# Latent attention heads in an order written by hand, modulation weights loaded a step ahead, zeros written by GpSimd

## The chip, the cores and the metric

The kernel runs on one core of a Trainium2 chip. The metric is the device time of that core in microseconds (us), from one launch to its end. The kernel before took 2492.16 us as the median of three runs (2489.03 to 2494.43).

Four engines share the work and run their own instruction streams side by side: TensorE (PE in the profile; its weight loads are listed as PEld), VectorE (DVE), ScalarE (ACT) and GpSimd (POOL). SyncE (SP) issues nearly all DMAs of this kernel, one after the other, in one queue. An engine works through its own stream in order and waits on semaphores for results of the others.

## The reference, cut to what matters

The program is a backbone of two layers over 256 latent tokens (x) and 256 context tokens (ctx) of width 2048, all in float32. Layer 0 has eight neighbourhood attention heads and eight latent attention heads side by side; layer 1 is a gated DeltaNet. The change lies in layer 0, in the last neighbourhood head, the latent heads, and the part of layer 1's modulation that is computed among them.

```python
def na_mla_layer(x, ctx, c, c_ctx, w_mod, b_mod, norm, w_in, rpb, q_norm, w_qb, kv_norm, w_kvb, w_out, update_ctx):
    ...
    hx = modulate(x, norm, sh[:, None], sc[:, None]) @ w_in
    hc = modulate(ctx, norm, sh_c, sc_c) @ w_in
    ...
    def mla_q(cq_t):                       # rank 512 -> 8 heads of 128 + 64 (rotary part)
        q = to_heads(rmsnorm(cq_t, q_norm) @ w_qb, MLA_HEADS)
        return q[..., :MLA_NOPE_DIM], q[..., MLA_NOPE_DIM:]
    def mla_kv(ckv_t):                     # rank 512 -> 8 heads of 128 (keys) + 128 (values)
        kv = to_heads(rmsnorm(ckv_t, kv_norm) @ w_kvb, MLA_HEADS)
        return kv[..., :MLA_NOPE_DIM], kv[..., MLA_NOPE_DIM:]
    ...
    o_mla = mla_latent_attention(qn, rope_2d(qr), kn, v=v, kr=rope_2d(kr), kn_c=kn_c, kr_c=kr_c, v_c=v_c)
    y = (jnp.concatenate([merge_heads(o_na), merge_heads(o_mla)], axis=-1) * jax.nn.silu(z)) @ w_out
def adaln_params(cond, w_mod, b_mod):      # shift, scale, gate of a layer
    return jnp.split(jax.nn.silu(cond) @ w_mod + b_mod, 3, axis=-1)
```

A latent head's score is the product of its 128 own channels plus the product of 64 rotary channels, whose keys all heads share. The latent queries attend to all 512 keys, the context queries to the 256 context keys alone.

## The kernel before

**Tiling.** T = 512 tokens (256 latent, 256 context) stand on the free axis, channels on the 128 partitions. A float32 product is made of three fp32r matmuls: high by high, high by low, low by high. `dense` issues them (L90, L91, L92), `split` makes the two parts of a weight tile (ScalarE's cast L77, VectorE's subtraction L78), and `product` (L365) is the same for scores and values. Weight tiles of 128x1024 (512 KB) are loaded by `load_raw` into a ring of four, and split into rings of three.

**A head** (`attend`): four transposes of v (pv, L371), then for the latent and the context queries, two blocks of 128 each: scores sp (L365), for a neighbourhood head a bias (L387), their maximum (L389), the exponential (L392) that also leaves the sum, its reciprocal and the scaling (L394, L395), transposes of the probabilities (pt, L398), the split of these into PT (high part on ScalarE, L357, low part on VectorE, L358), and the values po (L365), which are multiplied into the gate `go` (L405). PSUM holds two tiles "mm" for dense products, two "sp", a ring of two called "tr" that pv, pt and pp (the rotary permutation) share, one "st" (po) and one "pm" (pmod, pmt).

**The stage of the change.** After seven neighbourhood heads the kernel makes `craw` (the latent queries' and keys' inputs of rank 512 each) and the rotary keys, and the queries, keys and values of neighbourhood head 7 (`na7`). From `craw` it makes `cx`: high parts by ScalarE (L468) and low parts by VectorE (L469), eight of 128x512 each; `ch` is its first half. `cx` takes the memory of `hx`, the input of the dense products until then. Its second half, `qr`, holds the rotary queries of all latent heads, 64 partitions a head; the other 64 partitions are set to zero by ScalarE, as a copy of ones times 0 (L481, eight of 64x1024). Then come head 7's attention, four rotary blocks (`dense` of the weights `ab_wqr`, two tiles; then `roped`, L444 to L457: copy, permutation pp, three VectorE steps, two splits) and the eight latent heads 8 to 15, each with three dense products of 12 matmuls from 1536 columns of `ab_wb`, two tiles a head (queries and keys, 1024; values, 512). The tiles are called W0 and W1 (`ab_wqr`), W2 and W3 (head 8), W4 and W5 (head 9) and so on.

**The modulation.** Layer 1's modulation weights come as `mraw` tiles of 512 KB. Chunks 2, 3 and 8 have four groups each; a group is four matmuls (L141) of 32 rows of cond each, which write the four quarters of pmod and read two `mraw` tiles. The 12 groups are steps of a generator (`ahead`); the pool of its tiles is opened when `craw` has been freed. Chunk 9 follows behind the last dense product, and then comes the output projection.

**What sets the order.** The stage is written as straight code, and the framework's scheduler puts each engine's instructions into an order by its own estimate of times. Only the later DeltaNet stage has an order by hand (`manual_schedule`).

Of the kernel before, what the change touches and what calls it, by code (L numbers as in the profile page):

```python
# [8 lines left out]
F32 = mybir.dt.float32  # L9
F32R = mybir.dt.float32r  # L10
AF = mybir.ActivationFunctionType
# [6 lines left out]
S = 256  # L18
# [8 lines left out]
def trunk_kernel(ctx: ExitStack, tc: tile.TileContext, g):  # L27
# [10 lines left out]
    def mm_tile():  # L38
        return mmp.tile([128, T], F32, name="mm", tag="mm")
# [41 lines left out]
    def load_split(src, n=2048):  # L81
        return [split(load_raw(src[:, c:min(n, c + 1024)], min(1024, n - c)), min(1024, n - c))
                for c in range(0, n, 1024)]

    def dense(ps, w, off, kt, xh, xl, k0=0, sl=slice(0, T), first=True, last=True):
        for k in range(kt):
            c = off + k * 128
            wh, wl = w[c // 1024]
            c = slice(c % 1024, c % 1024 + 128)
            PE.matmul(ps, wh[:, c], xh[:, k0 + k, sl], start=first and k == 0, stop=False)  # L90
            PE.matmul(ps, wh[:, c], xl[:, k0 + k, sl], start=False, stop=False)  # L91
            end = PE.matmul(ps, wl[:, c], xh[:, k0 + k, sl], start=False, stop=last and k == kt - 1)  # L92
        return end.ins
# [225 lines left out]
    with tc.tile_pool(name="ab", bufs=2, reuse_waits="tile") as tp, \  # L319
# [87 lines left out]
        def keep(p, name):  # L407
            t = tp.tile([128, T], F32, name=name, tag=name, bufs=1)
            A.copy(t, p)
            return t  # L410
# [58 lines left out]
                V.tensor_tensor(ch[:, 8 + j], craw[:, j], ch[:, j].bitcast(F32), op=ALU.subtract)  # L469
        cr.release()  # L470
        mr = tc.alloc_tile_pool(name="mr2", bufs=2, reuse_waits="tile")
        ahead = later(mr, ((1, (2, 3, 8), 0),))

        rows = slice(0, 64), slice(64, 128)
        attend(*na7)
        w = load_split(g["ab_wqr"])
        for j in range(4):
            p = mm_tile()
            dense(p, w, j * 512, 4, ch, ch[:, 8:])
            for e in range(2):  # L480
                A.activation(qr[rows[1 - e], 4 * j + 2 * e:4 * j + 2 * e + 2],  # L481
                             ones[rows[1 - e], 0:1].unsqueeze(2).broadcast_to([64, 2, T]), AF.Copy, scale=0.0)
            roped(p, MLA_SCALE, [(rows[e], *[qr[rows[e], 4 * j + 2 * e + i] for i in range(2)]) for e in range(2)])
        for h in range(8):
            w = load_split(g["ab_wb"][h], 1536)
            o = []
            for j, (k0, name, sc) in enumerate(((0, "qT", MLA_SCALE), (4, "kT", 1.0), (4, "vT", 1.0))):
                p = mm_tile()
                last_mm = dense(p, w, j * 512, 4, ch, ch[:, 8:], k0)
                o.append(keep(p, name) if name == "vT" else parts(p, name, scale=sc))  # L490
            steps(ahead, 1)
# [948 lines left out]
```

## Time and profile before

| | busy us | share of the span | instructions |
|---|---|---|---|
| TensorE matmuls (PE) | 2428.2 | 97% | 16110 |
| TensorE weight loads (PEld) | 1963.1 | 79% | 16110 |
| VectorE (DVE) | 1762.8 | 71% | 3538 |
| ScalarE (ACT) | 1105.6 | 44% | 2446 |
| GpSimd (POOL) | 161.1 | 6% | 165 |

| | |
|---|---|
| median of 3 runs | 2492.16 us |
| profiled execution, its own time | 2493.04 us |
| its span, first to last instruction | 2491.2 us |
| HBM read, written | 356.94 MB, 35.39 MB |

A row of a group of instructions reads: line, engine, operation, result<-operands, the tile's partitions by elements, and the count; then busy us, mean ns of one, and the idle time of the engine ahead of them with what ended most of it. A row of the timeline begins with the start and the length in us; in brackets stands the wait ahead of it and what ended it. The whole span has one core, and its latent stage is the stretch from some 687 to 901 us.

### The profile page before, as it was taken

What the parts mean: (1) busy time and instruction counts of PE and PEld (TensorE: products, weight loads), DVE (VectorE), ACT (ScalarE), POOL (GpSimd) and SP (SyncE); (2) the same over time, 40 slices, a digit from 0 to 9 for tenths busy, and PEclk for the clock granted to TensorE, in tenths of its full rate; (3) what the DMA queues carried; (4) which work ended last, traced back from release to release, by engine and by line L of the source; (5) the groups of instructions that cost most, each with busy time, mean ns of one, the idle gap of its engine ahead of it and who ended that gap; (6) DMA issues with size and microseconds to landing.
All of it is one profiled execution on the core that took longest, in us unless ns stands there. A gap on an engine that the chain in (4) does not pass through costs nothing.

```text
span 2491.2 us, 42483 instructions
## 1 busy us (share of the span) xinstructions
PE 2428.2 (97%) x16110; PEld 1963.1 (79%) x16110; DVE 1762.8 (71%) x3538; ACT 1105.6 (44%) x2446; POOL 161.1 (6%) x165
## 2 busy tenths in 40 slices
PE   6999999999989999999999999999999999999998
PEld 4557888888858878858998989987777777777787
DVE  4654678883356687856998988885777777777765
ACT  4223332333254432257565655634444544445453
POOL 0000000000000000020011101000000000012000
PEclk9999999999999999999999999999999999999999
DMA  8872645542253366664665666774343333336454
GB/s 252 282 277 87 200 154 172 169 157 84 88 187 110 102 198 204 226 210 136 195 173 158 179 178 180 204 201 108 87 116 103 115 112 98 106 100 184 148 193 141
DMA packets 254940, 397.24 MB, mean 159 GB/s; under 512 B 122257, under 2 KB 163857, under 8 KB 254609
## 3 DMA queue, kind: packets, MB, share of 16 engines
q1 hardware_dynamic: 253584, 393.00, 52.0%
q8 instruction: 127, 2.08, 0.3%
q10 hardware_dynamic: 1152, 1.54, 0.2%
q14 instruction: 77, 0.62, 0.1%
HBM read 356.94 MB, written 35.39 MB: 157 GB/s over the span
## 4 chain that ended last, share of the span: by engine, by line
PE 88%; issue 5%; DMA 3%; DVE 2%; ACT 1%; SPq 0%; POOL 0%; DVEq 0%; POOLq 0%; ACTq 0%
PE mm L90 21%; PE mm L91 20%; PE mm L92 20%; PE pks L1033 3%; PE pmod L141 3%; PE ptr L1045 2%; PE sp L365 2%; PE mm L105 2%; PE po L365 1%; DMA mraw<-dn_wm 1%; PE ptr L1078 1%; PE psu L1064 1%; PE pks L1064 1%; PE pt L398 1%; PE mm L107 1%
## 5 line engine op out<-in xcount | busy, mean ns | idle before, releaser
L90 PE MATMUL mm<-hx,whi 128*128 128x512 f32 (+1 forms) x2304 | 843.7, 366 | 2.3 <-ACT t L664 2.2
L91 PE MATMUL mm<-hx,whi 128*128 128x512 f32 (+1 forms) x2304 | 820.6, 356 | 2.5 <-issue 2.5
L92 PE MATMUL mm<-hx,wlo 128*128 128x512 f32 (+1 forms) x2304 | 819.4, 356 | 0.6 <-DVE wlo L78 0.6
L77 ACT CAST whi<-raw 128x1024 fp32r<-128x1024 f32 (+2 forms) x346 | 338.6, 980 | 701.4 <-PE mm L91 502.3
L78 DVE TENSOR_TENSOR wlo<-raw,whi 128x1024 fp32r<-128x1024 f32 (+2 forms) x346 | 394.3, 1142 | 204.3 <-ACT whi L77 198.2
L90 PEld LDWEIGHTS mm<-hx,whi 128*128 128x128 f32 x2304 | 438.8, 190 | 106.3 <-issue 27.0
L92 PEld LDWEIGHTS mm<-hx,wlo 128*128 128x128 f32 x2304 | 438.6, 190 | 65.1 <-issue 4.2
L91 PEld LDWEIGHTS mm<-hx,whi 128*128 128x128 f32 x2304 | 438.8, 190 | 61.4 <-issue 9.2
L177 DVE SCALAR_TENSOR_TENSOR lacc<-mraw,cond,lacc 128x512 f32<-128x512 f32 x300 | 208.6, 746 | 0.7 <-DMA mraw<-dn_wm 0.7
L585 DVE SCALAR_TENSOR_TENSOR acc<-cin,taps,acc 128x508 f32<-128x508 f32 (+3 forms) x256 | 187.2, 731 | 20.3 <-ACT acc L576 17.2
L105 PE MATMUL mm<-hx,whi 128*128 128x512 f32 x480 | 173.1, 404 | 0.1
L1055 DVE SCALAR_TENSOR_TENSOR vl<-ptr,egm,vh 128x128 fp32r<-128x128 f32 x224 | 64.7, 346 | 95.1 <-ACT rf L1052 37.9
L107 PE MATMUL mm<-hx,wlo 128*128 128x256 f32 x457 | 128.4, 281 | 1.3 <-DVE wlo L1139 1.2
L141 PE MATMUL pmod<-mraw,cond 128*32 128x512 f32 (+2 forms) x640 | 98.4, 508 | 28.1 <-DMA mraw<-ab_wm 18.8
L1139 DVE TENSOR_TENSOR wlo<-raw,whi 128x1024 fp32r<-128x1024 f32 x84 | 102.5, 1221 | 13.5 <-ACT whi L1131 13.4
L105 PEld LDWEIGHTS mm<-hx,whi 128*128 128x128 f32 x480 | 88.9, 188 | 24.5 <-issue 5.0
L816 DVE SCALAR_TENSOR_TENSOR outer<-L,bv,X 128x31 f32<-128x31 f32 (+15 forms) x248 | 99.4, 401 | 6.4 <-POOL X L811 0.5
L90 PE MATMUL mm<-gx,whi 128*128 128x512 f32 x256 | 100.3, 394 | 3.4 <-DVE x1B L515 2.4
L599 ACT ACTIVATE ac<-acc 128x128 f32<-128x128 f32 x160 | 37.4, 300 | 144.2 <-DVE acc L585 144.1
L91 PE MATMUL mm<-gx,whi 128*128 128x512 f32 x256 | 100.4, 392 | 0.5 <-DVE gx L503 0.5
L92 PE MATMUL mm<-gx,wlo 128*128 128x512 f32 x256 | 99.8, 391 | 0.0
L1049 ACT ACTIVATE vh<-ptr,egm 128x128 fp32r<-128x128 f32 x224 | 71.3, 374 | 57.1 <-PE ptr L1045 55.2
(301 smaller groups left out, 3648.5 us busy)
## 6 DMA issues: line engine op xcount, KB each, us to landing
raw<-dn_w SPq DMA_DIRECT2D x194, 512.0 KB
mraw<-dn_wm SPq DMA_DIRECT2D x96, 512.0 KB
mraw<-ab_wm SPq DMA_DIRECT2D x88, 512.0 KB
raw<-ab_w SPq DMA_DIRECT2D x66, 512.0 KB
raw<-dn_wo SPq DMA_DIRECT2D x64, 512.0 KB
raw<-ab_wo SPq DMA_DIRECT2D x32, 512.0 KB
raw<-ab_w SPq DMA_DIRECT2D x32, 256.0 KB
spt<-sp SPq DMA_DIRECT2D x64, 128.0 KB
```

The lines of the kernel that those rows point to most:

```text
L77: A.copy(hi[:, :m], raw[:, :m])
L78: V.tensor_tensor(lo[:, :m], raw[:, :m], hi[:, :m].bitcast(F32), op=ALU.subtract)
L90: PE.matmul(ps, wh[:, c], xh[:, k0 + k, sl], start=first and k == 0, stop=False)
L91: PE.matmul(ps, wh[:, c], xl[:, k0 + k, sl], start=False, stop=False)
L92: end = PE.matmul(ps, wl[:, c], xh[:, k0 + k, sl], start=False, stop=last and k == kt - 1)
L105: PE.matmul(p2, wh[:, c], x[:, :, k0 + k], start=start, stop=stop)
L107: PE.matmul(p2[:, 0], wl[:, c], x[:, 0, k0 + k], start=False, stop=False)
L141: PE.matmul(pmod[32 * q:32 * q + 32, :m], cond[:, 4 * kg + q, :], raw[c // 1024][:, half + c % 1024:half + c % 1024 + m], start=kg == 0, s ...
L177: V.scalar_tensor_tensor(acc[:, s], raw[:, q], cond[:, k, s:s + 1], acc[:, s], op0=ALU.mult, op1=ALU.add)
L585: V.scalar_tensor_tensor(o3[:, :, i0:i1], p3[:, :, i0 + d:i1 + d], taps[:, ch, t:t + 1], o3[:, :, i0:i1], op0=ALU.mult, op1=ALU.add)
L816: V.scalar_tensor_tensor(o, L[:, rows, k:k + 1].broadcast_to([128, n, m]), bv[:, k:k + 1], X[:, k:k + 1, cols].broadcast_to([128, n, m]), ...
L1139: V.tensor_tensor(w, raws[j], h.bitcast(F32), op=ALU.subtract)
```

## The change

The diff replaces the heads' loop by an order written out by hand for TensorE, VectorE and ScalarE, from neighbourhood head 7's attention to the last latent head. `attend` becomes a generator, `attend_steps`, with eight pieces (two scores; v's transposes and the first turn of probabilities; and so on), and between its pieces stand the dense products of the next head, in blocks that can be stopped after each three matmuls. The rotary blocks stand between the pieces of head 7. The modulation is a generator of its own, `shifts_and_gate`, which issues the next group's two loads behind the four matmuls of one group, twice a head (slots 3 and 7); its tiles are in a ring of three. Weights are loaded up to four tiles ahead of their split. The latent queries of even heads lie in another tile (`lacc`), so that two heads' queries can exist at once. The zeros of `qr` are written by GpSimd, as ones minus ones, ahead of all this.

```diff
-        ahead = later(mr, ((1, (2, 3, 8), 0),))
+        def attend_steps(qT, kT, vT, h, bias=None, rope=None):
+            po = ps.tile([128, T], F32, name="po", tag="st", bufs=1)
...
+            scores(0)
+            yield
+            scores(1)
+            yield
+            pv = ps.tile([128, 4, 128], F32, name="pv", tag="tr", bufs=TR)
...
+            turn(0)
+            yield
+            scores(2)
+            yield
+            turn(1)
+            yield
+            values(0)
+            scores(3)
+            yield
+            turn(2)
+            yield
+            turn(3)
+            yield
+            values(1)
+        def weights():
+            while len(wraw) < min(len(WS), len(wsplit) + 4):
+                wraw.append(load_raw(*WS[len(wraw)]))
+            j = len(wsplit)
+            if j < len(WS):
+                wsplit.append(split(wraw[j], WS[j][1]))
+        def block(w, off, k0):
+            nonlocal last_mm
+            p = mm_tile()
+            for k in range(4):
+                last_mm = dense(p, [w], off + 128 * k, 1, ch, ch[:, 8:], k0 + k, first=k == 0, last=k == 3)
+                yield
+            return p
+        def rope_pair(j):
+            p = yield from block(wsplit[j // 2], j % 2 * 512, 0)
+            out = tp.tile([128, T], F32, name="rope", tag="rope", bufs=1)
+            A.mul(out, p, MLA_SCALE)
+            yield
+            pp = ps.tile([128, S], F32, name="pp", tag="tr", bufs=TR)
+            PE.matmul(pp, perm, out[:, :S], start=True, stop=True)
...
+        def queries(h):
+            p = yield from of_head(h, "q")
+            made[h, "q"] = parts(p, "qT", scale=MLA_SCALE) if h % 2 else parts(p, "lacc", scale=MLA_SCALE, pool=mr)
...
+        def shifts_and_gate():
+            def load(ch8, kg):
+                r = [mr.tile([128, 1024], F32, name="mraw", tag="mraw", bufs=3) for _ in range(2)]
+                for i in range(2):
+                    nc.sync.dma_start(r[i], g["dn_wm"][ch8, kg][:, 1024 * i:1024 * i + 1024])
+                return r
+            todo = [(c, kg) for c in (2, 3, 8) for kg in range(4)]
+            r = load(*todo[0])
+            yield
+            for n, (c, kg) in enumerate(todo):
...
+                for q in range(4):
+                    PE.matmul(pmod[32 * q:32 * q + 32], cond[:, 4 * kg + q, :], r[q // 2][:, q % 2 * 512:q % 2 * 512 + 512],
+                              start=kg == 0, stop=kg == 3, tile_position=(0, 32 * q))
...
+                if n + 1 < len(todo):
+                    r = load(*todo[n + 1])
+                yield
...
-        attend(*na7)
-        w = load_split(g["ab_wqr"])
-        for j in range(4):
...
-                A.activation(qr[rows[1 - e], 4 * j + 2 * e:4 * j + 2 * e + 2],
-                             ones[rows[1 - e], 0:1].unsqueeze(2).broadcast_to([64, 2, T]), AF.Copy, scale=0.0)
...
-            attend(*o, 8 + h, None, ([qr[:, 2 * h + i] for i in range(2)], [kr[:, i] for i in range(2)]))
-        steps(ahead)
+        for e in range(2):
+            for j in range(4):
+                one = ones[rows[1 - e], 0:1].unsqueeze(2).broadcast_to([64, 2, T])
+                P.tensor_tensor(qr[rows[1 - e], 4 * j + 2 * e:4 * j + 2 * e + 2], one, one, op=ALU.subtract)
+        for _ in range(3):
+            weights()
+        order = tc.manual_schedule(engines={mybir.EngineType.PE, mybir.EngineType.DVE, mybir.EngineType.Activation})
+        order.__enter__()
...
+        for h in range(-1, 8):
+            att = attend_steps(*now)
+            n = h + 1
+            fill = iter(())
+            for slot in range(1, 9):
+                next(att)
+                if n < 8:
+                    if h < 0:
+                        if slot == 1:
+                            fill = rope_pair(0)
+                            steps(fill, 5)
+                        elif slot == 2:
+                            steps(fill)
+                            fill = rope_pair(1)
+                            steps(fill, 5)
+                        elif slot == 3:
+                            steps(fill)
+                            steps(queries(0))
+                            weights()
...
+                        elif slot == 8:
+                            fill = rope_pair(3)
+                            steps(fill, 5)
+                            steps(fill)
+                            weights()
+                    else:
+                        if slot == 1:
+                            fill = queries(n)
+                            steps(fill, 2)
+                        elif slot == 2:
+                            steps(fill)
+                            fill = keys(n)
+                        elif slot in (3, 4):
+                            steps(fill, 1)
+                        elif slot == 5:
+                            steps(fill)
+                            fill = rest_of(n)
+                            weights()
+                        elif slot == 6:
+                            steps(fill, 1)
+                        elif slot == 7:
+                            steps(fill, 2)
+                            weights()
+                        elif slot == 8:
+                            steps(fill)
...
+                if slot in (3, 7):
+                    next(extra, None)
```

How the instructions stand on the engines, at the places that the prediction speaks of; a row is the line, the operation, result<-operands, the shape, and the count where a row repeats. GpSimd before, from craw's normalisation (the first two of L208) past layer 1's own (the third, and its modulated input, L243) to the DeltaNet stage's first work:

```order
L208 TENSOR_TENSOR rs<-ms,half 128x4 x3
L243 TENSOR_TENSOR hx<-mh,hx 128x512 x11
L798 MEMSET U 64x16x32
L799 MEMSET U 64x16x32
L810 MEMSET X 128x1024
```

and of the change, at the same place:

```order
L208 TENSOR_TENSOR rs<-ms,half 128x4 x2
L629 TENSOR_TENSOR cx<-ones 64x1024 x8
L208 TENSOR_TENSOR rs<-ms,half 128x4
L243 TENSOR_TENSOR hx<-mh,hx 128x512 x11
L1006 MEMSET U 64x16x32
L1007 MEMSET U 64x16x32
```

The eight zeros (L629) are new on GpSimd, behind the small steps of craw's normalisation. VectorE before, from the weight splits of W2 (wlo) through head 7's bias and maximum (sp, mx) to its first scaling (pr):

```order
L78 TENSOR_TENSOR wlo<-raw,whi 128x1024
L389 TENSOR_REDUCE mx<-sp 128x1
L387 TENSOR_TENSOR sp<-sp,bias 128x256
L469 TENSOR_TENSOR cx<-craw,cx 128x512 x3
L389 TENSOR_REDUCE mx<-sp 128x1
L469 TENSOR_TENSOR cx<-craw,cx 128x512 x5
L358 TENSOR_TENSOR vt<-pv,vt 128x512
L394 RECIPROCAL rc<-sm 128x1
L395 TENSOR_SCALAR pr<-pr,rc 128x512
```

and of the change, at the same place (L489 is the maximum there, L487 the bias, L494 and L495 the scaling, L569 the first step behind pp):

```order
L78 TENSOR_TENSOR wlo<-raw,whi 128x1024
L489 TENSOR_REDUCE mx<-sp 128x1
L469 TENSOR_TENSOR cx<-craw,cx 128x512 x8
L494 RECIPROCAL rc<-sm 128x1
L495 TENSOR_SCALAR pr<-pr,rc 128x512
L487 TENSOR_TENSOR sp<-sp,bias 128x256
L489 TENSOR_REDUCE mx<-sp 128x1
L494 RECIPROCAL rc<-sm 128x1
L495 TENSOR_SCALAR pr<-pr,rc 128x512
L569 TENSOR_TENSOR rtmp<-pp,ropet 128x256
```

All eight low parts of cx now stand ahead of the first scaling, and the step that reads pp stands behind two scalings. ScalarE before, behind the high parts of cx:

```order
L468 CAST cx<-craw 128x512 x8
L481 ACTIVATE cx<-ones 64x1024 x6
L357 CAST vt<-pv 128x512
L481 ACTIVATE cx<-ones 64x1024
L392 ACTIVATE pr,sm<-sp,mx 128x512
L481 ACTIVATE cx<-ones 64x1024
L392 ACTIVATE pr,sm<-sp,mx 128x512
```

and of the change:

```order
L468 CAST cx<-craw 128x512 x8
L492 ACTIVATE pr,sm<-sp,mx 128x512
L564 ACTIVATE rope<-mm 128x512
L492 ACTIVATE pr,sm<-sp,mx 128x512
L357 CAST cx<-rope 64x512 x2
L564 ACTIVATE rope<-mm 128x512
L357 CAST vt<-pv 128x512
```

The zeros (L481) are gone from ScalarE, and the exponential (L492) stands right behind the high parts, with the rotary copies (L564) between. TensorE of the change, behind the second rotary block:

```order
L92 MATMUL mm<-cx,wlo 128x512
L522 MATMUL pv<-ident,vT 128x128 x4
L504 MATMUL pt<-ident,pr 128x128 x4
L567 MATMUL pp<-rope,ropet 128x256
L90 MATMUL mm<-cx,whi 128x512
```

The tiles pv, pt and pp of the ring "tr" follow one another here without a dense product between; before, all four rotary blocks came behind head 7's first two score products and its pv.

More of the change, by code (lines that the diff above doesn't have):

```diff
@@ L484, in trunk_kernel @@
[L484 to L491, printed above, removed]
-            attend(*o, 8 + h, None, ([qr[:, 2 * h + i] for i in range(2)], [kr[:, i] for i in range(2)]))
@@ new lines, in trunk_kernel @@
+        WS = [(g["ab_wqr"][:, c:c + 1024], 1024) for c in (0, 1024)]
+        for h in range(8):
+            WS += [(g["ab_wb"][h][:, 0:1024], 1024), (g["ab_wb"][h][:, 1024:1536], 512)]
+        wraw, wsplit = [], []
+        def weights():
[11 more added lines that the diff above has]
+            return p
@@ new lines, in rope_pair @@
+        def rope_pair(j):
[5 more added lines that the diff above has]
+            PE.matmul(pp, perm, out[:, :S], start=True, stop=True)
+            t = tp.tile([128, S], F32, name="rtmp", tag="mtmp")
+            V.tensor_tensor(t, pp, sinT, op=ALU.mult)
+            V.tensor_tensor(out[:, :S], out[:, :S], cosT, op=ALU.mult)
+            V.tensor_tensor(out[:, :S], out[:, :S], t, op=ALU.add)
+            for e in range(2):
+                both(qr[rows[e], 4 * j + 2 * e], qr[rows[e], 4 * j + 2 * e + 1], out[rows[e]])
@@ new lines, in trunk_kernel, with of_head, keys, rest_of @@
+        made = {}
+        def of_head(h, name):
+            n = ("q", "k", "v").index(name)
+            return block(wsplit[2 + 2 * h + n // 2], n % 2 * 512, (0, 4, 4)[n])
+        def queries(h):
+            p = yield from of_head(h, "q")
+            made[h, "q"] = parts(p, "qT", scale=MLA_SCALE) if h % 2 else parts(p, "lacc", scale=MLA_SCALE, pool=mr)
+        def keys(h):
+            made[h, "k"] = yield from of_head(h, "k")
+        def rest_of(h):
+            made[h, "v"] = yield from of_head(h, "v")
@@ new lines, in trunk_kernel @@
+        next(extra)
+        now = na7
+        for h in range(-1, 8):
[17 more added lines that the diff above has]
+                            weights()
+                        elif slot == 4:
+                            steps(keys(0))
+                        elif slot == 5:
+                            fill = rope_pair(2)
+                            steps(fill, 5)
+                        elif slot == 7:
+                            steps(fill)
+                            steps(rest_of(0))
+                        elif slot == 8:
+                            fill = rope_pair(3)
+                            steps(fill, 5)
+                            steps(fill)
[9 more added lines that the diff above has]
+                            steps(fill, 1)
+                        elif slot == 5:
+                            steps(fill)
[3 more added lines that the diff above has]
+                            steps(fill, 1)
+                        elif slot == 7:
+                            steps(fill, 2)
+                            weights()
+                        elif slot == 8:
+                            steps(fill)
+                    if slot == 6:
+                        made[n, "k"] = parts(made[n, "k"], "kT")
+                    elif slot == 8:
+                        made[n, "v"] = keep(made[n, "v"], "vT")
+                if slot in (3, 7):
+                    next(extra, None)
+            steps(att)
+            if n < 8:
+                now = (made[n, "q"], made[n, "k"], made[n, "v"], 8 + n, None,
+                       ([qr[:, 2 * n + i] for i in range(2)], [kr[:, i] for i in range(2)]))
@@ L495, in trunk_kernel @@
+        steps(extra)
+        order.__exit__(None, None, None)
+        ahead = iter(())
         steps(later(mr, ((1, (9,), 0),), last_mm))
```

58 lines of the change are left out of this document (54 added, 4 removed).

## Prediction

> **What bounds the kernel now.** I read the page's busy shares first (TensorE 97% of the span), then busy time by stretches around the lines that the diff touches, then the timeline of each engine there. The change lies between 687 us, where the last neighbourhood head's score products start, and 901 us, where the last latent head's value products end.
>
> ```profile
> 687.00:742.00 55.00, 47.63 (x211) 26.38 (x210) 29.33 (x59) 30.44 (x50) 0.00 (x0) 0.97 0.53 178
> 742.00:861.00 119.00, 119.00 (x680) 98.35 (x683) 74.86 (x163) 54.05 (x124) 0.00 (x0) 1.00 0.31 100
> 861.00:901.00 40.00, 39.85 (x206) 28.49 (x198) 31.37 (x74) 18.04 (x50) 0.00 (x0) 1.00 0.60 190
> 950.00:1000.00 50.00, 50.00 (x230) 41.74 (x229) 40.76 (x63) 12.19 (x19) 0.00 (x0) 1.00 0.69 221
> ```
>
> The columns are the stretch, its length, then busy us of PE, PEld, DVE, ACT and POOL, the granted clock, DMA share and GB/s. Only the first 55 us, the opening, hold idle TensorE time (7.4 us). In the heads (742 to 861) TensorE never stands still, and neither does it later (950 to 1000), so what is won or lost here reaches the end of the span. "Busy" also counts matmuls that run badly. What waits and what runs badly is in these rows of the same stage:
>
> ```profile
> L141 PE MATMUL pmod<-mraw,cond 128*32 128x512 f32 x64 | 16.7, 641 | 6.1 <-DMA mraw<-dn_wm 6.1
> 700.60 3.12 PE L141 MATMUL pmod<-mraw,cond 128*32 128x512 f32 x8 [3.65 <-DMA mraw<-dn_wm]
> 732.83 1.86 PE L141 MATMUL pmod<-mraw,cond 128*32 128x512 f32 x8
> 756.53 1.06 PE L141 MATMUL pmod<-mraw,cond 128*32 128x512 f32 x8
> 741.73 1.20 PE L365 MATMUL sp<-kT,qT 128*128 128x512 f32 x4
> 860.30 0.39 PE L92 MATMUL mm<-cx,wlo 128*128 128x512 f32 x1
> ```
>
> The bound is thus TensorE, with 6.1 us of waits for modulation weights, and with modulation groups (four matmuls, 8 rows) that take 1.86 us when their two halves arrive apart and 1.06 when all four can run side by side.
>
> **The change, part by part.** I count from two anchors: the first score product of latent head 8 (741.73; 8 of the 12 modulation groups are then done), and the last dense product of head 15 (860.3). The sum is made against the profiled execution, 2493.04 us with a span of 2491.2; the median of the three runs, 2492.16, is 0.9 lower.
>
> *The opening, zeros left aside.* I walk the new order with these durations:
>
> ```profile
> 689.98 0.68 DVE L389 TENSOR_REDUCE mx<-sp 128x1 f32<-128x512 f32 x1
> 693.32 3.09 DVE L469 TENSOR_TENSOR cx<-craw,cx 128x512 fp32r<-128x512 f32 x5
> 705.22 0.49 DVE L395 TENSOR_SCALAR pr<-pr,rc 128x512 f32<-128x512 f32 x1
> 724.58 0.42 DVE L453 TENSOR_TENSOR rtmp<-pp,ropet 128x256 f32<-128x256 f32 x1 [2.28 <-PE pp L451]
> 725.37 0.43 DVE L455 TENSOR_TENSOR rope<-rope,rtmp 128x256 f32<-128x256 f32 x1
> 689.03 4.26 ACT L468 CAST cx<-craw 128x512 fp32r<-128x512 f32 x8
> 693.32 6.39 ACT L481 ACTIVATE cx<-ones 64x1024 fp32r<-64x1024 f32 x6
> 701.28 0.69 ACT L392 ACTIVATE pr<-sp,mx 128x512 f32<-128x512 f32 x1
> 725.88 1.26 ACT L357 CAST cx<-rope 64x512 fp32r<-64x512 f32 x2 [2.96 <-DVE rope L455]
> 722.33 0.60 ACT L449 ACTIVATE rope<-mm 128x512 f32<-128x512 f32 x1 [0.83 <-DVE cx L358]
> 706.51 0.40 PE L90 MATMUL mm<-cx,whi 128*128 128x512 f32 x1
> 709.02 0.39 PE L92 MATMUL mm<-cx,wlo 128*128 128x512 f32 x1
> ```
>
> A block of twelve matmuls takes 2.75 (eleven starts from 706.51 to 709.02). ScalarE loses its zeros (eight of 1.06, six of them in the row of 6.39), so its exponentials start at 693.3. VectorE does the eight low parts of cx in one go, 690.6 to 695.6 at 0.62 each. TensorE's first rope block waits for the first of them (691.3) and ends at 693.9; scores, pp, the second block and pv end at 698.2. Then it meets the ring of two PSUM tiles "tr": pt takes the tile that VectorE's rtmp must have read. That read stands behind the low parts, a scaling, a bias, a maximum, the second exponential (0.69 and its sum's read) and its scaling, at 698.6; pt starts at 699.1, a wait of 1.0. The second pp needs ScalarE's second rope copy, queued behind two casts of the first rope (until 701.2), and the tile of pv: 703.05, a wait of 3.4. Later v waits 1.9 for kT's low part to free its PSUM tile, the fourth pp 0.7 for its copy, and I allow 0.6 for semaphore gaps. Head 8 would start at 727.0.
>
> ```profile
> 700.00:704.00 4.00, 3.40 (x9) 0.72 (x10) 1.34 (x3) 3.95 (x8) 0.00 (x0) 0.65 0.79 294
> ```
>
> Behind a wait of like length the clock fell to 0.65, and eight rows took 3.12 in place of 1.86; I charge 1.2. Head 8 starts at 728.2, a **lead of 13.5**. [...]
>
> *The first change of heads.* W4 (queries and keys of head 9) is now split behind the fourth rope pair's casts: after that pair's last matmul come its copy, pp, three VectorE steps (1.2), two casts (1.3) and then the split itself,
>
> ```profile
> 727.17 1.04 ACT L77 CAST whi<-raw 128x1024 fp32r<-128x1024 f32 x1
> 728.25 1.23 DVE L78 TENSOR_TENSOR wlo<-raw,whi 128x1024 fp32r<-128x1024 f32 x1 [0.31 <-ACT whi L77]
> ```
>
> so that the low half is there 6.2 us after it, where TensorE asks at 3.0. With what can run in between: **+2.7**.
>
> *The heads.*
>
> ```profile
> 811.67 0.28 PE L365 MATMUL po<-PT,vt 128*128 128x256 f32 x1
> 828.08 0.28 PE L365 MATMUL po<-PT,vt 128*128 128x256 f32 x1
> 711.00 0.59 ACT L357 CAST PT<-pt 128x512 fp32r<-128x512 f32 x1 [4.77 <-PE pt L398]
> 711.62 0.69 DVE L358 TENSOR_TENSOR PT<-pt,PT 128x512 fp32r<-128x512 f32 x1 [3.92 <-ACT PT L357]
> ```
>
> One head without modulation takes 16.4 (828.08 - 811.67), and the same matmuls stand in the new order. Ten modulation groups are left for the heads, against four before. Both halves are loaded a step (9 us) ahead, so each should run four wide, 1.1 with its switch: 10.9 against 5.2, **+5.7**. The new order is tight in two places. Six matmuls (1.4) stand between the second transposes and the first values, which need 0.59 and 0.69 behind an exponential and its scaling: short by 0.2. Three matmuls stand between the last transposes and the last values, with a 1.23 weight split ahead of VectorE's low part: short by 0.4, by 1.6 in the one head with a split and no modulation. Five heads at 0.6 and one at 1.8: **+4.8**. On SyncE five modulation loads wait ahead of a weight load, but seven weight loads precede them; cost 0, and without that lead one landing, some 4 us (3.65 in the row of 700.60).
>
> *The last head.* Six value products of head 14 are left behind the last dense product, where before there were eighteen and four transposes (-1.7); the loads of chunk 9 find fewer matmuls to hide behind (taken as +1.5): **-0.2**.
>
> So far -13.5 + 2.7 + 5.7 + 4.8 - 0.2 = **-0.5 us**: the order alone comes out even.
>
> *The zeros on GpSimd.* Eight subtractions, 64x1024 each, start when hx has been read for the last time, 687.9, just when VectorE does W2's low half (from 688.85) and the eight low parts of cx, each with two inputs in SBUF. This stage has no GpSimd work before; later stages do:
>
> ```profile
> L820 POOL TENSOR_TENSOR X<-X,bv 128x1024 f32<-128x1024 f32 x7 | 14.4, 2051 | 95.2 <-DVE X L818 95.2
> L243 POOL TENSOR_TENSOR hx<-mh,hx 128x512 fp32r<-128x512 f32 x22 | 30.7, 1399 | 197.8 <-ACT mh L241 197.6
> L1185 POOL TENSOR_TENSOR hx<-gin,hx 128x1024 fp32r<-128x1024 f32 x3 | 7.7, 2581 | 3.3 <-ACT hx L1184 3.3
> 1416.77 0.74 DVE L585 SCALAR_TENSOR_TENSOR acc<-cin,taps,acc 128x510 f32<-128x510 f32 x1
> 2238.41 2.37 POOL L1185 TENSOR_TENSOR hx<-re,hx 128x1024 fp32r<-128x1024 f32 x1 [6.74 <-ACT hx L1184]
> 2240.74 2.83 POOL L1185 TENSOR_TENSOR hx<-gin,hx 128x1024 fp32r<-128x1024 f32 x1
> L585 DVE SCALAR_TENSOR_TENSOR acc<-cin,taps,acc x2: 1539/2145/2751, 2239.8 to 2241.4; 128x508 f32<-128x508 f32 x2
> 2239.46 0.42 DVE L1083 TENSOR_TENSOR rf<-rf,ptr 128x256 f32<-128x256 f32 x1 [1.15 <-PE ptr L1078]
> ```
>
> Alone L585 takes 0.74. Beside two GpSimd instructions in a row it took 1.54 and 2.75: the first ended 0.55 behind the end of the first GpSimd instruction (2240.78), the second 0.55 behind that of the second (2243.57), and the second GpSimd instruction was itself longer by the one that had got in between. They take turns, whole instructions at a time. L1083, which reads one input from PSUM, ran through (0.42). So each low part of cx should wait for one zero. At 2.05 each (L820, the same 1024 elements a partition): W2's low half waits 1.1, the first low part 1.45 (a maximum from PSUM covers some), six more 2.05 each, less 0.5 of spacing: **+14.3**. Everything up to the second pp hangs on the end of that chain (710 in place of 695.6), so it goes to the path whole. By L243 (1.40) it is 9.5, by L1185 (2.58) 18; I take L820's as the nearest, and keep both ends. [...]
>
> Sum: -0.5 + 14.3 = +13.8, 2506.8 against the profiled execution, **2506** against the median.
>
> **The rivals.** [...]
>
> *Faster.* The zeros cost nothing, and TensorE comes to the values late enough: of a head's 16.4 about 15.9 are matmuls at their own pace, and if the other 0.5 lies just in the two tight places, their 4.8 go: -5.3, 2487. It decides only if the zeros cost under 0.3 in all. Against: TensorE's gaps are spread.
>
> *The modulation still runs two wide*, as its halves are two DMAs with waits of their own: 12 x 0.8 = +9.6 on top of the forecast, 2516. Against: a step's lead of 9 us, where landing took 4.
>
> **How the numbers follow.** Forecast (zeros block VectorE) 0.63, at 2506, with 2501 to 2511 by the bounds of a zero; zeros free 0.16, at 2491.7; faster 0.17, at 2487 or less; two wide 0.04. About 0.2% (5 us) is what a measurement of this kernel can tell from no change. Slower by over that: 0.63 + 0.04, less 0.01 for a forecast that falls short, 0.66; same 0.17; faster 0.17. The range goes down through the free zeros to 2488 and up to 2514 (bound of 18, with some of the two-wide case).
>
> **What would show it.** In the changed profile: the eight cx<-craw parts on VectorE at 2.5 us apart instead of 0.62, ending near 710; eight GpSimd instructions of 2 to 2.7 each from 688; TensorE waiting on VectorE's cx and then on rtmp until 717; ScalarE free of zeros; modulation groups of 1.1; head 8 near 742 to 743; short waits for PT ahead of the values; W4's wait at the first change of heads. It is wrong if the low parts keep their 0.62, if the zeros start after 696, or if heads with hand order take under 16.4.

## The result, and the profile after

The changed kernel takes 2513.43 us (median of 4 runs, 2510.32 to 2515.22) against 2491.62 for the kernel before (4 runs, 2489.03 to 2494.43): 21.8 us slower, ratio 1.008 with a 95% interval of 1.0067 to 1.0093. The forecast was +13.8 us, 2506, in a range of 2488 to 2514. The direction was right and the difference 8 us larger than forecast: the time lies above the 2511 that the forecast gave as its own upper bound for a zero, and 0.6 us inside the range.

The busy time by stretches of the changed kernel, with the columns of the same view in the prediction (stretch, length, PE, PEld, DVE, ACT, POOL, granted clock, DMA share, GB/s):

```profile
687.00:742.00 55.00, 39.87 (x166) 28.57 (x165) 36.24 (x49) 18.25 (x36) 18.43 (x8) 0.81 0.26 86
742.00:757.00 15.00, 12.85 (x61) 9.18 (x60) 8.88 (x19) 6.98 (x15) 0.00 (x0) 0.89 0.20 66
764.00:881.00 117.00, 111.95 (x638) 86.14 (x637) 68.73 (x148) 47.71 (x109) 0.00 (x0) 1.00 0.40 135
881.00:921.00 40.00, 34.97 (x162) 23.06 (x163) 28.58 (x68) 17.92 (x48) 0.00 (x0) 0.91 0.51 167
```

Before, TensorE stood still only in the opening (7.4 us of 55) and was busy through the heads and up to 901 us. Now 15.1 us of the opening are idle, at a mean clock of 0.81, and the heads (5.0 of 117) and the tail (5.0 of 40) have gaps too.

Four marks on TensorE's timeline tell where the difference arises. Of the kernel before (the other two, 741.73 and 860.30, stand in the prediction), head 7's first score and the projection's last product:

```profile
687.63 1.52 PE L365 MATMUL sp<-kT,qT 128*128 128x512 f32 x6
...
1065.55 0.39 PE L92 MATMUL mm<-gx,wlo 128*128 128x512 f32 x1
```

and of the changed kernel, all four:

```profile
689.30 0.84 PE L365 MATMUL sp<-kT,qT 128*128 128x512 f32 x3
...
741.92 0.86 PE L365 MATMUL sp<-kT,lacc 128*128 128x512 f32 x3
...
881.67 0.40 PE L92 MATMUL mm<-cx,wlo 128*128 128x512 f32 x1
...
1092.86 0.39 PE L92 MATMUL mm<-gx,wlo 128*128 128x512 f32 x1
```

| stretch | before | after | difference | forecast |
|---|---|---|---|---|
| start to head 7's first score | 687.6 | 689.3 | +1.7 | 0 |
| opening, to head 8's first score | 54.1 | 52.6 | -1.5 | +0.8 |
| heads, to the last cx product | 118.6 | 139.8 | +21.2 | +13.2 |
| tail, to the last gx product | 205.3 | 211.2 | +5.9 | -0.2 |
| the rest of the span | 1425.6 | 1420.5 | -5.1 | 0 |
| span | 2491.2 | 2513.4 | +22.2 | +13.8 |

The first and the last row are outside the change's stage; more on them below.

**The zeros.** The changed kernel's timeline of GpSimd and of VectorE, at the start of the opening:

```profile
689.61 18.51 POOL L629 TENSOR_TENSOR cx<-ones 64x1024 fp32r<-64x1024 f32 x8 [37.57 <-PE mm L92]
...
690.52 2.06 DVE L78 TENSOR_TENSOR wlo<-raw,whi 128x1024 fp32r<-128x1024 f32 x1
692.50 0.68 DVE L489 TENSOR_REDUCE mx<-sp 128x1 f32<-128x512 f32 x1
693.10 16.16 DVE L469 TENSOR_TENSOR cx<-craw,cx 128x512 fp32r<-128x512 f32 x8
```

The eight low parts of cx stand 2.3 us apart, where five took 3.09 before, and end at 709.3 (forecast 710). The maximum ahead of them reads PSUM and keeps its 0.68. TensorE's longest waits from 685 to 725 in the changed kernel, by who ended them (sum, times, longest):

```profile
PE mm L91 <- DVE cx L469: 5.0, 4, 3.1
PE pt L504 <- DVE rtmp L569: 4.5, 1, 4.5
PE pp L567 <- DVE vt L358: 3.7, 1, 3.7
```

These are the forecast waits: the rope block at the pace of the low parts, pt for rtmp (which stands behind that chain), then the second pp.

**The heads.** The same view from 725 to 870:

```profile
PE po L365 <- DVE PT L358: 2.5, 4, 0.9
PE pmod L607 <- DVE mod L621: 1.8, 2, 0.9
PE mm L90 <- ACT whi L77: 1.6, 1, 1.6
PE pp L567 <- ACT rope L564: 0.7, 1, 0.7
PE mm L92 <- DVE wlo L78: 0.5, 1, 0.5
```

The first row is the values that wait for PT, the third and fifth are W4 at the first change of heads. The second was not in the forecast: pmod and pmt share one PSUM tile, so a new chunk's first group waits until VectorE has read the last chunk's transposes.

**The tail.** TensorE's waits from 860 to 920 before, and the longest from 870 to 935 in the changed kernel:

```profile
PE mm L90 <- DVE x1B L515: 2.4, 1, 2.4
PE mm L90 <- ACT gx L502: 1.0, 1, 1.0
PE mm L91 <- DVE gx L503: 0.5, 1, 0.5
```

```profile
PE pmod L141 <- DMA mraw<-dn_wm: 3.1, 2, 2.6
PE mm L91 <- DVE gx L711: 2.2, 2, 1.8
PE mm L90 <- DVE x1B L723: 2.1, 1, 2.1
PE mm L90 <- ACT gx L710: 1.2, 2, 1.0
```

New are the waits for chunk 9's weights (3.1). Those for the first casts of gx, the projection's input, have grown (3.4, from 1.5), and the wait for x1B stood there before. The clock of 0.91 in the last row of the stretches above, against 1.00 before, is worth up to 3.6 us of the 40 more; this is an estimate.

### The profile page after: what moved, and what is told of

It reads as the page before. It is cut to its first block, busy times and chain, and to the rows that moved or that the text cites. A ratio compares the mean times of both kernels' runs of the same rounds, so it can differ in the third digit from the quotient of the medians.

```text
span 2513.4 us, 42447 instructions
## 1 busy us (share of the span) xinstructions
PE 2430.1 (97%) x16110; PEld 1964.9 (78%) x16110; DVE 1775.7 (71%) x3538; ACT 1099.2 (44%) x2440; POOL 177.3 (7%) x173
## 4 chain that ended last, share of the span: by engine, by line
PE 85%; issue 5%; DVE 4%; DMA 3%; ACT 2%; SPq 0%; POOL 0%; DVEq 0%; POOLq 0%; ACTq 0%
PE mm L90 21%; PE mm L91 20%; PE mm L92 19%; PE pks L1241 3%; PE pmod L141 2%; PE ptr L1253 2%; PE sp L365 2%; PE mm L105 2%; PE po L365 1%; PE ptr L1286 1%; DMA mraw<-ab_wm 1%; DMA mraw<-dn_wm 1%; PE psu L1272 1%; PE pks L1272 1%; PE mm L107 1%
## 5 line engine op out<-in xcount | busy, mean ns | idle before, releaser
L141 PE MATMUL pmod<-mraw,cond 128*32 128x512 f32 (+2 forms) x544 | 76.7, 487 | 26.1 <-DMA mraw<-ab_wm 19.8
```

The lines of the kernel that those rows point to most:

```text
L141: PE.matmul(pmod[32 * q:32 * q + 32, :m], cond[:, 4 * kg + q, :], raw[c // 1024][:, half + c % 1024:half + c % 1024 + m], start=kg == 0, s ...
```

## The experiments

Each was timed against the kernel before on the same chip; the kernel before had a median of 2492.82 (29 runs) beside e1 to e4, 2491.11 (27 runs) beside e5 to e9, and 2492.22 (13 runs) beside e10 to e13. A signed difference below is to that median; the changed kernel's is +21.8.

### e1: the zeros as memsets

```diff
-                P.tensor_tensor(qr[...], one, one, op=ALU.subtract)
+                P.memset(qr[...].bitcast(F32), 0.0)
```

> The changed kernel, with the eight zeros of qr still on GpSimd and at the same place, but as memsets, which read nothing. [...] Rival 1 (any GpSimd instruction with SBUF as its target holds VectorE off): the low parts stay above 1.5 each and the time at 2508 or more. Rival 2 (the loss of the opening is in the hand order, not in the zeros): the low parts fall to 0.62 but head 8 still starts after 738.

Measured: 2496.61 (12 runs), +3.8, ratio 1.0016 (1.0002 to 1.0029). If GpSimd and VectorE take turns where both read, low parts of 0.62 each and 2499 to 2503 were to be expected; the time is some 2 us below that. Its timeline of GpSimd, VectorE and TensorE:

```profile
688.40 7.31 POOL L628 MEMSET cx<- 64x1024 f32 x8 [37.55 <-PE mm L92]
...
689.33 1.22 DVE L78 TENSOR_TENSOR wlo<-raw,whi 128x1024 fp32r<-128x1024 f32 x1
...
691.06 4.90 DVE L469 TENSOR_TENSOR cx<-craw,cx 128x512 fp32r<-128x512 f32 x8
...
688.11 0.84 PE L365 MATMUL sp<-kT,qT 128*128 128x512 f32 x3
...
728.50 0.86 PE L365 MATMUL sp<-kT,lacc 128*128 128x512 f32 x3
```

The same engine writes the same bytes at the same place beside the same VectorE work, and the low parts are back at 0.61 each, W2's low part at 1.22. The opening takes 40.4 in place of 52.6: writing the zeros by subtraction and not by memset cost 12.2 us there, and 18.0 in the medians (+21.8 became +3.8), of which 3.9 are a shorter tail (207.3 in place of 211.2). The heads take the same 139.7, so their +21.2 is the order's own. Both rivals fall. In this pair of runs VectorE's subtractions of two SBUF inputs took 2.3 a turn (low parts of cx) and 2.06 (W2's low part) beside GpSimd's subtraction, which reads SBUF, and 0.61 and 1.22 beside its memset, which only writes there.

### e2: the zeros on ScalarE

```diff
-                P.tensor_tensor(qr[...], one, one, op=ALU.subtract)
...
                 if slot in (3, 7):
                     next(extra, None)
+                if h < 0:
+                    zero(slot - 1)          # A.activation(..., AF.Copy, scale=0.0), as before
```

> The changed kernel, with the eight zeros of qr on ScalarE as before, one behind each piece of head 7. No GpSimd work is left beside the low parts of cx. Theory (turns between GpSimd and VectorE): low parts of 0.62 each, ending near 697; head 8's first score near 729 to 732, since ScalarE has 8.5 us more to do among the rotary copies; time 2500 to 2504. Rival (the opening's loss is in the hand order): head 8 starts after 738 and the time stays above 2508.

Measured: 2502.83 (6 runs), +10.0, ratio 1.0042 (1.0026 to 1.0058). The low parts take 0.61 each again, and head 8 starts at 730.7. Its opening is 2.3 longer than e1's (42.7). Half of that is seen as a wait: ScalarE's zeros stand among the steps that free the ring, and the second pp, TensorE's longest wait there, waits 4.8 where e1's waits 3.6. The rest of the 6.2 between the medians of e1 and e2 isn't traced.

```profile
PE pp L567 <- DVE vt L358: 4.8, 1, 4.8
```

### e3: the kernel before, with GpSimd's zeros alone

```diff
-                A.activation(qr[...], ones[...].broadcast_to([64, 2, T]), AF.Copy, scale=0.0)
+                P.tensor_tensor(qr[...], one, one, op=ALU.subtract)     # ahead of head 7's attention
```

> The kernel before, with one part of the change alone: the zeros on GpSimd as ones minus ones. Theory (turns): the low parts of cx take 2.3 us each and end near 708 in place of 696.4; TensorE's first rotary block, 694.5 to 709 before, runs at their pace; the exponentials start some 8 us sooner, which gives part back: time 2496 to 2504, slower than before by 5 to 12. Rival (the zeros cost nothing, and freeing ScalarE gains): 2487 to 2490.

Measured: 2497.44 (12 runs), +4.6, ratio 1.0021 (1.0008 to 1.0035). The low parts as one row of the view by line (shortest, median and longest in ns), and two of TensorE's waits from 685 to 755 (the largest sum there, 4.9, is for modulation weights, as before):

```profile
L469 DVE TENSOR_TENSOR cx<-craw,cx x8: 679/2373/2377, 694.0 to 709.2; 128x512 fp32r<-128x512 f32 x8
```

```profile
PE pt L398 <- DVE pr L395: 4.3, 1, 4.3
PE mm L91 <- DVE cx L469: 2.8, 1, 2.8
```

The same turns, at a lower price: the scheduler's order has head 7's products to put between, and ScalarE is free earlier. So the edit is a loss by itself too: 4.6 in the medians, where in the hand order, whose every step up to the second pp hangs on that chain, e1 showed 18.0. The two don't compare one to one, since e3 also holds what a freer ScalarE gains, and no run separates that.

### e4: the last head left to the scheduler

```diff
-        for h in range(-1, 8):
+        for h in range(-1, 7):
...
-        steps(extra)
         order.__exit__(None, None, None)
+        attend(*now)
+        steps(extra)
```

> The changed kernel, with the order by hand ended behind head 14's pieces, and the last head, 15, left to the framework's scheduler as before. Theory of the tail (gx, the projection's input, takes cx's memory, so its casts wait for the last product that reads cx; in the hand order that is head 15's fourth score, which stands behind value products and, in TensorE's row, behind chunk 9's loads): the four scores come early again, the casts of gx start within 4 us of them, the first gx product near 897 in place of 902.6, and from the last cx product to the last gx product it takes 206 to 208 in place of 211.2; time 2506 to 2510. Rival (the tail's loss is chunk 9's loads alone, with few matmuls to hide behind): less than 2 us saved.

Measured: 2499.89 (12 runs), +7.1, ratio 1.0031 (1.0019 to 1.0044); 14.7 less than the changed kernel's +21.8, twice the most that was expected. From the last cx product to the last gx product it takes 197.3 in place of 211.2, 8 less even than before. Of these 8, 1.7 is work that the heads have taken over and 3.3 are waits (3.9 before, 0.6 here); the rest isn't traced. Of all TensorE's waits from 883 to 935 one is left:

```profile
PE mm L90 <- DVE x1B L724: 0.6, 1, 0.6
```

### e5: both

> Both edits together: the zeros as GpSimd memsets (alone 2496.6) and the last head left to the scheduler (alone 2499.9), against 2513.4 for the changed kernel. Theory (two separate causes, one in the opening, one in the tail): the savings add, 16.8 + 13.5, and the time is 2481 to 2486, faster than before by 7 to 11; head 8's first score near 728.5 and from the last cx product to the last gx product some 197 us. Rival (both edits remove the same loss, or the second hides behind a DMA once the first is gone): 2490 or more.

Measured: 2488.25 (12 runs), -2.9, ratio 0.9985 (0.9975 to 0.9995). From head 7's first score to the projection's last product it takes 378.1, level with the 377.9 before (197.4 in the tail, as e4), so the gain in the medians lies behind the projection (see "What lies outside the stage"). The time misses the theory's 2481 to 2486, and the savings add in part: 24.7 of 18.0 + 14.7. Of the overlap, 3.9 is the tail, which was shorter already in e1.

### e6: the modulation as before

```diff
-        extra = shifts_and_gate()
-        next(extra)
+        extra = later(mr, ((1, (2, 3, 8), 0),))
```

> The kernel of e5, with the modulation's groups made as before (loads written at the step itself and not a step ahead, transposes in the same step as the fourth group), at the same places of the heads. Theory (loading a step ahead makes each group run four wide, 1.0 in place of 1.86): groups go back to 1.5 to 1.9 us each and wait for their loads, 12 times 0.5 to 2 us, so 6 to 20 us slower than e5. Rival (the loads run ahead anyway, since SyncE has little else to issue and the ring of tiles sets when they land): within 3 us of e5, groups of 1.0 to 1.1.

Measured: 2493.65 (11 runs), +2.5, ratio 1.0000 (0.9988 to 1.0013). A group of e6 on the timeline, and TensorE's longest wait from 725 to 870:

```profile
749.40 1.06 PE L141 MATMUL pmod<-mraw,cond 128*32 128x512 f32 x8
```

```profile
PE pmt L150 <- DVE macc L147: 4.3, 3, 1.4
```

At 5.4 slower than e5 it falls between the two forecasts. The rival was right on the loads: the groups run four wide at 1.06 and wait for no DMA, though the load is written at the step itself. So the written lead isn't what keeps the halves together; the distance between groups may be, but no run changes that alone. The 4.3 are transposes that wait for VectorE's copy of the chunk, which stands in the same step there. At the last gx product, counted from head 7's first score, e6 is 2.1 behind e5; the rest of the 5.4 between the medians isn't explained.

### e8 and e9: the places that the hand order leaves tight

```diff
                         elif slot == 3:
-                            steps(fill)
                             steps(queries(0))
+                            steps(fill)
...
-                            fill = rope_pair(3)
-                            steps(fill, 5)
-                            steps(fill)
+                            late = rope_pair(3)
+                            steps(late, 4)
                             weights()
+                            steps(late, 1)          # the rest behind head 8's first score
```

> The kernel of e5, with two steps of the hand order moved: head 8's queries (12 products) ahead of the second rotary permutation pp, and the split of W4 right behind the last rotary products, with that block's pp, three VectorE steps and casts moved behind head 8's first score. Theory (TensorE waits 3.6 for pp's tile and 1.6 + 0.5 for W4 with its clock falling behind each): both waits go, head 8's first score comes 3 to 4 us sooner and its second score 2 to 3 us sooner again; 4 to 7 us faster than e5. Rival (the same VectorE and ScalarE steps are only late for the next product that needs them): the waits reappear ahead of PT or kT, and the time stays within 2 us of e5.

e8 measured 2486.35 (9 runs), -4.8, ratio 0.9983 (0.9972 to 0.9994). Head 8 starts 5.8 sooner after head 7's first score than in e5, W4's waits are gone, and the second pp waits 0.9:

```profile
PE pp L567 <- DVE vt L358: 0.9, 1, 0.9
```

At the last gx product, counted the same way, 8.3 us are gained on e5, but only 1.9 in the medians: in the profiled execution 5.4 are lost again by 1126 us, in waits for modulation weights (6.2, where e5 has 3.2) and for ScalarE (4.0, where e5 has 2.2).

e9 takes pmt one piece sooner, and the next head's weight split into slot 6.

> The kernel of e8, with two more moves: the transposes of a modulation chunk (pmt) one piece sooner than the next chunk's first group, which waits 0.9 for their reading, and the split of the next head's first weight tile one piece sooner (slot 6 in place of 7), since it stands on VectorE ahead of the low part of PT for which the last values wait 0.6. Theory: 3 waits of 0.9 and 6 of 0.6 go, 4 to 6 us faster than e8. Rival (the split now delays the earlier PT by as much): 1 to 3 us.

e9 measured **2477.12** (5 runs, 2475.34 to 2483.5), -14.0, ratio 0.9946 (0.9933 to 0.9958): the lowest time of all versions. Up to the last gx product it gains 1.3 on e8, no more. The other 7.4 us between the two profiles lie behind it (1418.7 us to the end, where e8 takes 1426.1), and neither move touches that stretch, so the 9.2 between the medians isn't a measure of the moves. In the heads the waits behind pmt are gone, but the weight split moved for nothing, and the values' waits grew, from 2.9 in e8 to

```profile
PE po L365 <- DVE PT L358: 3.6, 5, 1.1
```

### e10 and e11: which part of the last head's order costs

e10, on e1: the last head's third and fourth score products (not their softmax) behind the second.

```diff
             scores(1)
+            if early:                 # h == 7
+                multiply(2)
+                multiply(3)
```

> The kernel with memsets (e1, 2496.6; from the last cx product to the last gx product 207.3 us) and the hand order kept for all heads, but in the last head the matmuls of the third and fourth scores stand right behind those of the second; their maxima and exponentials stay where they were. Chunk 9's loads stay behind the last cx product. Theory A (gx takes cx's memory, and its casts wait for the last product that reads cx): the casts of gx start within 3 us of the fourth score, products of gx fill the last head's waits, 198 to 201 us between the marks, time 2486 to 2490. Theory B (the tail waits for chunk 9's loads): TensorE still stands behind them, 204 or more, time 2494 or more.

e11, on e1: chunk 9 in the heads.

```diff
-            todo = [(c, kg) for c in (2, 3, 8) for kg in range(4)]
+            todo = [(c, kg) for c in (2, 3, 8, 9) for kg in range(4)]
...
-        steps(later(mr, ((1, (9,), 0),), last_mm))
```

> The kernel with memsets (e1, 2496.6) and the hand order kept, scores of the last head late as there, but chunk 9's four groups made among heads 14 and 15 like the others, and not behind the last cx product. Theory A (gx waits for cx's memory): the heads get 4 to 5 us longer, the tail loses four groups (7.4 at two wide) but stands bare ahead of gx, with waits for the softmax of some 4 to 6 us; time 2493 to 2498. Theory B (the tail waits for chunk 9's loads): no such waits, 196 to 198 us between the marks, time 2486 to 2491.

e10 took 2507.20 (5 runs, ratio 1.0056, 1.0039 to 1.0072) and e11 2512.80 (5 runs, 1.0083, 1.0066 to 1.0099), +15.0 and +20.6 where e1 has +3.8. In e10 gx starts early, as theory A says (casts from 879.06, 0.1 behind the last score), and yet the tail takes 212.2. That is within the numbers of theory B, but not by its cause: chunk 9's weights make 1.5 of the waits. In e11 the softmax waits of theory A come, but larger, and the time lies 15 us above its range. TensorE's longest waits in e10 from 864 to 925, and three of those in e11 from 870 to 935:

```profile
PE pt L509 <- DVE pr L500: 4.6, 2, 4.0
PE mm L90 <- ACT gx L717: 2.0, 1, 2.0
PE pmod L141 <- DMA mraw<-dn_wm: 1.5, 2, 1.1
```

```profile
PE pt L504 <- DVE pr L495: 6.1, 1, 6.1
PE po L365 <- ACT PT L357: 3.0, 1, 3.0
PE po L365 <- DVE PT L358: 1.9, 1, 1.9
```

In e10 90 gx products are through before the last two turns of probabilities, of which the second then waits 4.0 with nothing to run; in e11 the softmax of the last head waits with nothing to run from its start, as chunk 9's groups were what lay between. So the tail's loss is neither gx's memory nor chunk 9's loads alone. What fits all of these runs, though none shows it alone, is this: behind the last cx product TensorE has a limited stock of other work (chunk 9's four groups, and the 71 to 90 gx products that run ahead of the last values in these kernels); the last head's chain of softmax steps needs it spread between its pieces, and the hand order has no fill there.

### e12 and e13: further moves

e12, on e8: pmt early, VectorE's copy of a finished chunk behind the last low part of PT, chunk 9 in the heads. e13, on e12: both scores of head 7 ahead of the first rope block.

```diff
-                    V.tensor_copy(acc, pmod)
...
+                    yield "turn"                     # resumed in slot 8
+                    V.tensor_copy(acc, pmod)
```

> Memsets, the last head left to the scheduler, the opening's steps as in e8, pmt one piece early as in e9, the weight split back in slot 7, chunk 9 among the heads, and VectorE's copy of a finished modulation chunk (0.69) behind the last low part of PT in place of ahead of it. Theory (that copy is what the last values of every second head wait for, since a chunk ends there): the waits of 0.85 to 1.02 at heads 8, 10 and 12 fall under 0.3; chunk 9 runs four wide in the heads; 2 to 6 us faster than e9's 2477. Rival (the waits come from the weight split, and chunk 9's groups cost in the heads what they save in the tail): 2475 to 2480.

> The kernel of e12, with both scores of head 7 ahead of the first rotary block, and the second block's products ahead of the first pp. Theory (TensorE's first two waits of 1.4 for cx, high and low part, are partly covered by the second score's 0.7, and the first pp no longer stands close behind its copy): 0.5 to 2 us faster than e12. Rival (the chain copy, pp, VectorE, casts of the first block starts later and the later blocks wait for it): the same or up to 2 us slower.

e12 measured 2482.45 (5 runs, -9.8, ratio 0.9958, 0.9942 to 0.9974), outside both of its forecasts, and e13 2483.60 (8 runs, -8.6, ratio 0.9971, 0.9956 to 0.9987), as its rival said. In e12, TensorE's waits from 725 to 870:

```profile
PE pt L398 <- DVE pr L395: 1.9, 2, 1.4
PE mm L90 <- ACT gx L715: 0.9, 1, 0.9
PE po L365 <- DVE PT L358: 0.3, 1, 0.3
```

The third row fits the theory that the copy was what the values waited for (2.9 in e8, now 0.3). The first two may be the price of chunk 9 in the heads: the last head has less between its pieces, even with the scheduler. The interval of e12 overlaps e9's, so which of the two is faster isn't settled. e13's first product waits 0.6 less for cx but its pp waits 1.6 for the rope copy; nothing is gained.

## Why the prediction was right, and where it fell short

| step of the prediction | forecast | the runs show |
|---|---|---|
| the opening's lead, without the zeros | -13.5 | -13.7 (40.4 in e1 against 54.1 before) |
| zeros that block VectorE's low parts | +14.3 (9.5 to 18) | +12.2 in the opening (e1), 18.0 in the medians |
| W4 at the first change of heads | +2.7 | 2.1 of waits, and 15 us at a clock of 0.89: 1.7 more, an estimate |
| six more modulation groups in the heads | +5.7 | 5.2 start to start, and 1.8 of waits behind pmt |
| values that wait for PT | +4.8 | 2.5 shown as waits; from start to start 6.0 lost to a pace of 0.117, where before 0.7 was lost: 5.4 |
| the last head | -0.2 | +5.9; mended by e4 |

The main step, that the zeros block VectorE, is shown by e1, e2 and e3 together. Its size was near: a zero took 2.3 with its turn, the forecast had counted 2.5.

The walk of the opening was right to 0.2 us in sum, and part of that is luck. In e1, two waits that the walk had counted, 1.0 for pt and 1.9 for v, do not appear. Instead the first rope block waits for the high parts of cx as well as for the low ones, and then eleven of its products take 4.15 us, where the pace of 0.23 needs 2.5. TensorE's waits there, from the view of e1 from 685 to 725:

```profile
PE mm L90 <- ACT cx L468: 1.2, 1, 1.2
PE mm L91 <- DVE cx L469: 1.1, 1, 1.1
```

Behind the second pp's wait of 3.6 products started 0.43 apart in place of 0.23 (from 705.65 to 708.64); the slower pace cost 1.8, where 1.2 was charged.

What made the forecast 8 us short is in three places. **A term of -1.7 was counted on one side only**: the twelve value products and four transposes that leave the tail are done in the heads (120 value products there, where before there were 108), and were credited to the tail and not charged there. **The tail** was mis-sized: 1.5 for chunk 9's loads "with fewer matmuls to hide behind", where with the 1.7 set right 7.6 were lost; e4 takes them away, and e10 and e11 narrow down why without settling it. **Small waits in the heads** were missed: pmt's reader (1.8), and the clock that fell behind W4's waits (1.7). The heads came out 8.0 longer than forecast: 1.7 + 1.8 + 1.7 of it are named here, the three forecast terms together came 0.5 lower (2.1 + 5.2 + 5.4, forecast 13.2), and the other 3.3 are not traced. With the tail's 6.1 more, the opening's 2.3 less and 3.4 less outside the stage, that is the difference of 8.4 between +22.2 and +13.8. That the time still fell inside the range is luck too: in the stage 25.6 us were lost, and the 3.4 that came back lie where the change does nothing that the forecast spoke of.

The rivals: zeros that cost nothing fell (e1), and with them the faster one, which also needed the values' waits to go. The order alone, put at -0.5, looks near by its median and was not: e1, the order with zeros that block nothing, is 3.8 slower than before, but 9.5 slower in the stage, with 7.0 made up behind it. Only with the tail mended too (e5) is the stage level with before. Groups that run two wide fell: the ten in the heads took 1.06 or 1.07 each, though not for the reason of the change (e6).

**What lies outside the stage.** The first 1.7 us are waits before 75 us, where TensorE's order is the same in both kernels: 1.0 more for modulation weights and 0.6 more for the first tile of hx. They differ from execution to execution (head 7's first score came between 687.1 and 689.9 in the profiles of e1 to e13). The 5.1 that come back later are mostly at one place in the DeltaNet stage. TensorE's longest wait there, before and after:

```profile
PE pu L851 <- issue: 2.8, 2, 2.3
```

```profile
PE pu L1059 <- issue: 0.6, 1, 0.6
```

The granted clock behind it was 0.75 from 1316 to 1322 before, and 1.00 at the same products after (1340 to 1346). Between the same two products (some 225 and 275 us behind the last gx product) the changed kernel and all experiments but e3 take 4.1 to 5.4 us less than before; only before and e3, which have the scheduler's order in the heads, lose them. Why issue stalls there stays open.

So every signed difference above but e3's holds some 5 us that do not come from the stage. From head 7's first score to the last gx product the profiles take 377.9 before, 403.6 for the changed kernel, 387.4 in e1, 378.1 in e5, 369.8 in e8 and 368.5 in e9: of e9's gain about 9 us are the stage's.

## What to carry to other kernels

That GpSimd was idle did not make the work moved to it free: VectorE's low parts of cx, subtractions of two SBUF inputs, took 2.3 a turn beside GpSimd's subtractions and 0.61 beside its memsets, 12 us in the opening. Look at what VectorE runs beside such work, and try a form that reads nothing. An order by hand that fills the pieces of one step with the next step's products must say what fills the last step; here that place was worth 10 us (the tail of 207.3 in e1, 197.4 in e5). And when a term takes work out of one stretch, charge it in the stretch that receives it.

## What the runs showed of the hardware that was not expected

A GpSimd memset of 64x1024 took 0.91 (7.31 for eight in e1), and VectorE's low parts beside it 0.61 each, as in e2 with no GpSimd work there; the subtraction of the same size beside the same work took 2.3 a turn. And the clock fell on short waits. In the changed kernel, around W4's two waits (1.62 and 0.53, with two matmuls between), by the columns of the stretches above:

```profile
743.00:745.00 2.00, 0.47 (x3) 0.04 (x1) 1.37 (x2) 1.95 (x4) 0.00 (x0) 1.00 0.00 0
745.00:747.00 2.00, 1.38 (x4) 0.85 (x5) 1.93 (x3) 0.52 (x2) 0.00 (x0) 0.75 0.00 0
747.00:749.00 2.00, 2.00 (x6) 1.59 (x5) 0.87 (x3) 0.78 (x2) 0.00 (x0) 0.50 0.68 225
749.00:751.00 2.00, 2.00 (x9) 1.61 (x8) 0.65 (x1) 0.00 (x0) 0.00 (x0) 0.90 0.13 45
```

It was at 0.50 while TensorE was busy again, for some 3 us by these rows, though no single wait was longer than 1.62. The prediction had charged the clock only behind one wait of some 3.4.
